# A decoder layer in fp32: partial sums of the first projections added by DVE out of PSUM instead of by POOL, in fewer and larger rounds of k-tiles, with shift and scale made for four k-tiles at a time

## The chip, the cores and the metric

The kernel runs on one core of a Trainium2 chip. The metric is the device time of one execution in microseconds; less is better. The engines are named as the profile names them: PE (matmuls), PEld (its weight loads), DVE (vector), ACT (scalar), POOL (GpSimd) and SP, whose queue issues nearly all loads.

## The reference

One layer (DEPTH is 1) of a decoder trunk over 256 tokens of width 2048. The part around the change:

```python
mod = (jax.nn.silu(c) @ w_ada[l] + b_ada[l]).reshape(B, N_MOD, 1, D)
sh1, sc1, gt1, sh2, sc2, gt2 = (mod[:, j] for j in range(N_MOD))
h = rmsnorm(x, g_mix[l]) * (1.0 + sc1) + sh1
z = h @ w_in[l]          # 2048 x 16392, cut into the inputs of three mixers and three gates
```

c is one vector, so the modulation is a product of a vector with a 2048 x 12288 matrix, 100 MB of which all has to be read; shift sh1 and scale sc1 (33 MB) must be there before h is. The products z feed an mLSTM, a differential attention and a stick-breaking attention; their outputs go through one projection each, are gated and summed, and go through an output projection. A gated MLP with a causal convolution follows. All is fp32, and every large weight matrix is read once.

## The kernel before

**Precision.** PE multiplies in an fp32 format that it rounds (fp32r). Each operand is therefore split into a high part, which ACT makes by a cast (line 305, `hi`), and a low part, which DVE makes as raw minus high (line 307, `lo`); a product takes three matmuls: high by high, high by low, low by high. Every weight tile passes through this split. One split covers two k-tiles: 128 x 1024 elements where a chunk has 512 columns, 128 x 880 where it has 440 ("wide" and "narrow" below). The split tiles have four buffers each, of two k-tiles.

**Modulation.** DVE multiplies each row block of w_ada by its element of silu(c) and accumulates (`ada_mac`, lines 204 and 206); sums over the partitions are then made on PE (`partition_sums`, tile pm, line 218) and DVE. `ada_first(k0)` makes shift and scale for two k-tiles of 128 features: 4 steps, each with two loads of 512 KB (shift and scale side by side in one raw tile) and four accumulations of 512 columns. Then `make_h` builds hh and hl, the split h for these k-tiles, on ACT (lines 400 and 355) and DVE (line 356). The result for k-tiles 0 and 1 comes first, the others run beside the projections.

**Rounds.** The first 13 chunks of columns of w_in (the inputs of the stick-breaking and differential attentions: four chunks of 512 with features on the partitions, "F", line 339; two of 512 and seven of 440 with tokens on the partitions, "T", line 337) are multiplied before all of h is there. So the 16 k-tiles are cut into rounds. `partial(ci, kt0, kt1)` does chunk ci for k-tiles kt0 to kt1: load, split, matmuls into two PSUM banks (`gemm`; there are three banks for it), and the result goes to its place in SBUF. In the first round ACT writes it there (line 464). In later rounds before, ACT copies the bank to a tile `part` (line 461) and POOL adds that to the place (line 466). In the last round, 12 to 16 (8 to 16 for two postponed chunks), DVE adds straight out of PSUM (line 468). The rounds before: 0 to 2 and 2 to 4 for all 13 chunks; 4 to 6 and 6 to 8 for ten; 4 to 8 for the other three; 8 to 12 for eleven; then the last.

**Order.** After each chunk `tick()` advances the queue of modulation steps by `rates["ada"]` (0.4, later 0.9 in this stage) and side work (attention) by another rate. If h for a round is not made when the round is written, `partial` pumps the queue until it is; `drain(ada)` ends it after round 8 to 12. The order on each engine is worked out from this by a planner that simulates times; the engines themselves run their queues in order. Loads of modulation and weights go through SP's one queue in order. Raw tiles of two k-tiles of w_in have three buffers of 512 KB of their own; raw tiles of four k-tiles and those of `ada_first` share three buffers of 1 MB.

After the last round come the gates, the mixers as side work beside the remaining projections, the branches, the output projection and the MLP.

Of the kernel before, what the change touches and what calls it, by code (L numbers as in the profile page):

```python
# [10 lines left out]
F32 = mybir.dt.float32  # L11
F32R = mybir.dt.float32r
AF = mybir.ActivationFunctionType
ALU = mybir.AluOpType
# [3 lines left out]
P = 128  # L18
S = 256
NT = S // P  # L20
D = 2048
KD = D // P
# [17 lines left out]
def kernel(  # L40
# [6 lines left out]
    nc = tc.nc  # L47
    x2d, out2d = x[0], out[0]
    w_ada, w_in, w_out, w_up, w_down = w_ada[0], w_in[0], w_out[0], w_up[0], w_down[0]
# [4 lines left out]
    rawp = ctx.enter_context(tc.tile_pool(name="rawp", bufs=3))  # L54
# [6 lines left out]
    adaps = ctx.enter_context(tc.tile_pool(name="adaps", bufs=1, space=PSUM))  # L61

    def slot(i, name):
        n = NT * MH * (MDH + 1) + 8 if i == 2 else 2048
        return slots.tile([P, n], F32, tag=f"s{i}", name=name)
# [4 lines left out]
    def wide(name):  # L70
        return tmp.tile([P, 512], F32, tag="wide", name=name, bufs=3)
# [7 lines left out]
    V, A, T = nc.vector, nc.scalar, nc.tensor  # L79


    ident = const.tile([P, P], F32, name="ident")
    make_identity(nc, ident)
    ones = const.tile([P, P], F32, name="ones")
# [36 lines left out]
    ccol, gmix_c = colsA[:, 0:16], colsA[:, 16:32]  # L121
    bsh1_c, bsc1_c, bsh2_c, bsc2_c = (colsA[:, 32 + 16 * i:48 + 16 * i] for i in range(4))
# [51 lines left out]
    ada = deque()  # L174
    state = {"ada": 0.0, "side": 0.0, "split": None, "load": None, "hold": None, "h": 0, "started": False}
# [13 lines left out]
    rates = {"ada": 0.0, "side": 1.0}  # L189
# [9 lines left out]
    def ada_mac(accs, raw, kt0, nk):  # L199
        for k in range(nk):  # L200
            kt = kt0 + k
            acc = accs[kt % len(accs)]
            if kt < len(accs):
                V.tensor_scalar(acc, raw[:, k, :], ccol[:, kt:kt + 1], None, ALU.mult)  # L204
            else:
                V.scalar_tensor_tensor(acc, raw[:, k, :], ccol[:, kt:kt + 1], acc, ALU.mult, ALU.add)  # L206

    def partition_sums(accs):

        pm = adaps.tile([P, 512], F32, tag="adaps", name="pm")  # L210
        if len(accs) > 1:
            for i, acc in enumerate(accs):
                for k in range(4):
                    T.matmul(pm[:, k:k + 1], lhsT=acc[:, k * P:(k + 1) * P], rhs=ones[:, 0:1],
                             start=k + i == 0, stop=i == len(accs) - 1, skip_group_check=True)
            return pm
        for k in range(4):
            T.transpose(pm[:, k * P:(k + 1) * P], accs[0][:, k * P:(k + 1) * P], ident)  # L218
        sums = tmp.tile([P, 4], F32, tag="sums", name="sums")
        V.tensor_reduce(sums, pm.rearrange("p (k f) -> p k f", k=4), AX.X, ALU.add)  # L220
        return sums

    def ada_first(k0):

        accs = [adap.tile([P, 512], F32, tag="acc", name="acc", bufs=2)]
        if k0 == 0:
            accs.append(sidewide("acc2"))
        for q in range(4):
            raw = rawp.tile([P, 4, 512], F32, tag="raw", name="raw")
            step = 2 if k0 == 0 and q == 3 else 4  # L230
            for j in range(0, 4, step):
                for i in range(2):
                    r0, c0 = q * 512 + j * P, i * D + k0 * P
                    with tc.issue_after(state["load"].ins) if k0 else nullcontext():
                        load = nc.sync.dma_start(raw[:, j:j + step, i * 256:(i + 1) * 256],
                                                 w_ada[r0:r0 + step * P, c0:c0 + 256].rearrange("(k p) f -> p k f", p=P))
            if k0 == 0:
                state["load"] = load
            with tc.issue_after(state["first"].ins) if k0 == 2 and q == 0 else nullcontext():
                ada_mac(accs, raw, 4 * q, 4)  # L240
            yield
        pm = partition_sums(accs)
        ks = slice(k0, k0 + 2)
        V.tensor_tensor(b1[:, ks], pm[:, 0:2], bsh1_c[:, ks], ALU.add)  # L244
        V.tensor_tensor(a1[:, ks], pm[:, 2:4], bsc1_c[:, ks], ALU.add)
        V.tensor_tensor(a1[:, ks], a1[:, ks], gmix_c[:, ks], ALU.mult)
        make_h(k0, k0 + 2)

    def ada_late(comp, g):

# [10 lines left out]
    def ada_columns(comp, bcol, dst, gcol=None):  # L261
        for g in range(4):
            for acc in ada_late(comp, g):
                yield
            pm = partition_sums([acc])
            ks = slice(4 * g, 4 * g + 4)
            V.tensor_tensor(dst[:, ks], pm[:, 0:4], bcol[:, ks], ALU.add)
            if gcol is not None:
                V.tensor_tensor(dst[:, ks], dst[:, ks], gcol[:, ks], ALU.mult)
# [17 lines left out]
    a1 = const.tile([P, KD], F32, name="a1")  # L287
    b1 = const.tile([P, KD], F32, name="b1")
# [101 lines left out]
    def make_h(kt0, kt1):  # L390
        ts = []
        for kt in range(kt0, kt1):
            t = small("ht")
            ts.append(t)
            if kt0 == 0:
                A.activation(hh[:, kt, :], xnT_k(kt), AF.Identity, scale=a1[:, kt:kt + 1], bias=b1[:, kt:kt + 1])
                V.tensor_scalar(t, xnT_k(kt), a1[:, kt:kt + 1], b1[:, kt:kt + 1], ALU.mult, ALU.add)
                state["split"] = V.tensor_tensor(hl[:, kt, :], t, hh[:, kt, :].bitcast(F32), ALU.subtract)
            else:
                A.activation(t, xnT_k(kt), AF.Identity, scale=a1[:, kt:kt + 1], bias=b1[:, kt:kt + 1])  # L400
                state["split"] = split(hh[:, kt, :], hl[:, kt, :], t)
        if kt0 == 0:
            state["first"] = state["split"]
        state["h"] = kt1
# [44 lines left out]
    def shaped(src, dst):  # L449
        return src.rearrange("p (a b) -> p a b", a=dst.shape[1]) if len(dst.shape) == 3 else src  # L450

    def partial(ci, kt0, kt1, on_pool=True):
        orient, col0, n, dest, scale = first[ci]
        while state["h"] < kt1:
            pump(ada, 1)
        pin = kt0 == 0 and ci == 1
        acc = gemm(orient, hact, w_in, 0, col0, n, kt0, kt1, hold=state["first"] if pin else None, hold_all=pin)
        for b in range(2):
            if kt0 and on_pool:
                t = wide("part")  # L460
                A.activation(t[:, :n], acc[b][:, :n], AF.Copy, scale=scale)  # L461
            for cs, d in dest(b):
                if kt0 == 0:
                    A.activation(d, shaped(acc[b][:, cs], d), AF.Copy, scale=scale)
                elif on_pool:
                    nc.gpsimd.tensor_tensor(d, d, shaped(t[:, cs], d), ALU.add)
                else:
                    V.scalar_tensor_tensor(d, shaped(acc[b][:, cs], d), scale, d, ALU.mult, ALU.add)
        tick()

    NC, NE = 10, 11
    ada.extend(ada_first(k0) for k0 in range(2, KD, 2))
    rates["ada"] = 0.4
    for ci in range(13):
        partial(ci, 0, 2)
    for ci in range(13):
        partial(ci, 2, 4)
    with tc.issue_after(state["load"].ins):
        late_vectors()
    for ci in range(NC):  # L480
        partial(ci, 4, 6)
    for ci in range(NC):
        partial(ci, 6, 8)
    rates["ada"] = 0.9
    for ci in range(NC, 13):
        partial(ci, 4, 8)
    for ci in range(NE):
        partial(ci, 8, 12)
# [305 lines left out]
    ada.append(ada_rest())  # L794
    rates["side"] = 2.4
    for ci in range(13):
        partial(ci, 12 if ci < NE else 8, 16, on_pool=False)
        if ci == 5:
            side.append(stick())

# [18 lines left out]
    for ch in range(2):  # L819
        acc = gemm("T", hact, w_in, 0, C_MO + ch * 512, 512, 0, KD)  # L820
# [5 lines left out]
    for ch in range(2):  # L826
        acc = gemm("T", hact, w_in, 0, C_MV + ch * 512, 512, 0, KD)
# [5 lines left out]
    for t, col0, f0 in ((mqT, C_MQ, 0), (mkT, C_MK, 8)):  # L833
        for ch in range(2):
            acc = gemm("F", hact, w_in, 0, col0 + ch * 512, 512, 0, KD)
# [40 lines left out]
    for ch in range(4):  # L876
        acc = gemm("T", mact, w_out, 0, ch * 512, 512, 0, KD)
        cs = slice(ch * 512, (ch + 1) * 512)
        for tt in range(NT):
            t = wide("t512")  # L880
# [15 lines left out]
        for k2 in range(2):  # L896
            pb = bank("px2")
            for tt in range(NT):
                for j in range(2):
                    k = 4 * ch + 2 * k2 + j  # L900
                    T.transpose(pb[:, j * S + tt * P:j * S + (tt + 1) * P], x2[tt][:, k * P:(k + 1) * P], ident)
            for j in range(2):
                k = 4 * ch + 2 * k2 + j
                A.activation(xT[k // 8][:, (k % 8) * S:(k % 8 + 1) * S], pb[:, j * S:(j + 1) * S], AF.Copy,
                             scale=a2[:, k:k + 1])
# [5 lines left out]
    for k in range(0, KD, 2):  # L911
# [3 lines left out]
        for j in range(2):  # L915
            b = b2[:, k + j:k + j + 1]
# [9 lines left out]
    for half, (c0, c1) in enumerate(((0, 6), (6, NCH))):  # L926
        ath = [slots.tile([P, 8, S], F32R, tag=f"s{i}", name=f"ath{i}") for i in (0, 3, 4)]
        atl = [slots.tile([P, 8, S], F32R, tag=f"s{i}", name=f"atl{i}") for i in (5, 6, 7)]
        for ch in range(c0, c1):
# [18 lines left out]
            i, j0 = (ch - c0) // 2, ((ch - c0) % 2) * 4  # L948
            for b in range(2):
                V.tensor_tensor(y[b], accu[b], y[b], ALU.mult)  # L950
                ks = slice(j0 + 2 * b, j0 + 2 * b + 2)
# [4 lines left out]
        for n in range(4):  # L956
            acc = gemm("T", act, w_down, c0 * 512, n * 512, 512, 0, 4 * (c1 - c0))
            cs = slice(n * 512, (n + 1) * 512)
            for tt in range(NT):
                t = wide("t512")  # L960
# [34 lines left out]
```

## Time and profile before

| | |
|---|---|
| three runs | 1870.74 us median (1869.49 to 1871.23) |
| profiled execution | 1869.62 us, span 1867.8 us, mean granted clock 0.990 |
| PE, weight loads | busy 1799.6 us (96%), 1684.9 us (90%) |
| DVE | busy 1365.7 us (73%) |
| ACT | busy 924.6 us (49%) |
| POOL | busy 180.5 us (10%) |
| DMA | 423.75 MB, 227 GB/s over the span |

The times of the instructions come from the profiled execution, whose own time is 1.8 us more than its span, the distance from its first to its last instruction. Matmuls are pipelined, so that the busy time of PE is more than its work. Idle time of an engine costs only where the engine that sets the pace waits for it.

### The profile page before, as it was taken

To read this page: it belongs to the slowest core of one execution; us is meant where nothing else is said; L and a number is where in the kernel's file an instruction comes from. 1 tells how busy PE (TensorE), PEld (TensorE's weight loads), DVE (VectorE), ACT (ScalarE), POOL (GpSimd) and SP (SyncE) were. 2 spreads that over 40 slices of the span, in tenths; PEclk is the share of its full clock that TensorE was granted. 3 is DMA by queue.
4 is the path that set the end of the run, shared out by engine and by line. 5 is a ranking of instruction groups with operands and counts; after the bars stand their busy time and mean duration, and the time that the engine had idled before them with its cause. 6 is when DMAs were issued, how large, how long until landed. Compare 5 with 4: busy or idle time off the path is not lost.

```text
span 1867.8 us, 30413 instructions
## 1 busy us (share of the span) xinstructions
PE 1799.6 (96%) x12433; PEld 1684.9 (90%) x12433; DVE 1365.7 (73%) x1687; ACT 924.6 (49%) x1226; POOL 180.5 (10%) x146
## 2 busy tenths in 40 slices
PE   6887789999999999999999999999999999999998
PEld 5776679999988999999999879999998889999987
DVE  6999997888888688686887567777774545555554
ACT  6655444666656464453444455444443334444432
POOL 0588652000000000000000000000000000000000
PEclk9988999999999999999999999999999999999999
DMA  9867786667677657666898547777765565555563
GB/s 317 268 211 230 247 273 209 217 231 237 205 254 268 233 187 252 215 235 240 308 306 284 196 151 242 253 249 261 250 212 198 186 197 186 181 181 181 185 221 113
DMA packets 232105, 423.75 MB, mean 227 GB/s; under 512 B 8928, under 2 KB 56349, under 8 KB 231453
## 3 DMA queue, kind: packets, MB, share of 16 engines
q1 hardware_dynamic: 230141, 417.56, 66.4%
q8 instruction: 97, 1.59, 0.4%
q0 software_dynamic: 544, 2.11, 0.3%
q10 hardware_dynamic: 1280, 2.14, 0.3%
q14 instruction: 43, 0.35, 0.1%
HBM read 419.68 MB, written 2.10 MB: 226 GB/s over the span
## 4 chain that ended last, share of the span: by engine, by line
PE 86%; DVE 7%; DMA 3%; issue 2%; ACT 1%; SPq 0%; DVEq 0%; ACTq 0%
PE gp L339 56%; PE gp L337 26%; DVE lo L307 3%; DVE acc L206 3%; DMA raw<-in_w_ada_dram 2%; DMA raw<-in_w_in_dram 1%; ACT hi L305 0%; PE psc L593 0%; DMA x<-in_x_dram 0%; PE pxt L387 0%; PE pm L218 0%; DVE acc L204 0%; ACT x L381 0%; PE pr L284 0%; DVE b L244 0%
## 5 line engine op out<-in xcount | busy, mean ns | idle before, releaser
L307 DVE TENSOR_TENSOR lo<-raw,hi 128x1024 fp32r<-128x1024 f32 (+1 forms) x608 | 760.1, 1261 | 365.4 <-ACT hi L305 346.1
L305 ACT CAST hi<-raw 128x1024 fp32r<-128x1024 f32 (+1 forms) x608 | 622.9, 1037 | 675.9 <-PE gp L339 359.3
L339 PE MATMUL gp<-hh,hi 128*128 128x256 f32 x2688 | 700.1, 285 | 5.9 <-ACT hi L305 2.0
L339 PE MATMUL gp<-hl,hi 128*128 128x256 f32 x2688 | 700.3, 285 | 0.0
L339 PEld LDWEIGHTS gp<-hh,hi 128*128 128x128 f32 x2688 | 519.0, 193 | 8.4 <-ACT hi L305 2.7
L339 PE MATMUL gp<-hh,lo 128*128 128x256 f32 x2688 | 514.8, 284 | 10.5 <-DVE lo L307 10.5
L339 PEld LDWEIGHTS gp<-hl,hi 128*128 128x128 f32 x2688 | 519.6, 193 | 0.7 <-DVE hl L918 0.2
L339 PEld LDWEIGHTS gp<-hh,lo 128*128 128x128 f32 x2688 | 408.2, 193 | 12.3 <-DVE lo L307 11.8
L206 DVE SCALAR_TENSOR_TENSOR acc<-araw,colsA,acc 128x512 f32<-128x512 f32 x240 | 178.9, 745 | 5.7 <-DMA araw<-in_w_ada_dram 3.8
L337 PE MATMUL gp<-hi,hh 128*128 128x440 f32 (+1 forms) x416 | 161.5, 388 | 8.9 <-ACT part L461 4.7
L337 PE MATMUL gp<-hi,hl 128*128 128x440 f32 (+1 forms) x416 | 158.3, 381 | 0.0
L337 PE MATMUL gp<-hi,atl 128*128 128x512 f32 x352 | 136.9, 389 | 0.0
L337 PE MATMUL gp<-hi,ath 128*128 128x512 f32 x352 | 136.9, 389 | 0.0
L206 DVE SCALAR_TENSOR_TENSOR acc<-raw,colsA,acc 128x512 f32<-128x512 f32 x119 | 125.6, 1063 | 6.5 <-DMA raw<-in_w_ada_dram 4.4
L337 PE MATMUL gp<-lo,hh 128*128 128x440 f32 (+1 forms) x416 | 117.2, 384 | 10.3 <-DVE lo L307 10.3
L337 PE MATMUL gp<-lo,ath 128*128 128x512 f32 x352 | 105.8, 389 | 0.0
L337 PEld LDWEIGHTS gp<-hi,hh 128*128 128x128 f32 x416 | 79.9, 192 | 24.9 <-ACT part L461 7.3
L337 PEld LDWEIGHTS gp<-lo,hh 128*128 128x128 f32 x416 | 78.5, 191 | 24.2 <-DVE lo L307 14.1
L337 PEld LDWEIGHTS gp<-hi,hl 128*128 128x128 f32 x416 | 79.8, 192 | 10.0
L337 PEld LDWEIGHTS gp<-lo,ath 128*128 128x128 f32 x352 | 66.1, 188 | 13.8
L337 PEld LDWEIGHTS gp<-hi,ath 128*128 128x128 f32 x352 | 66.1, 188 | 13.7
L337 PEld LDWEIGHTS gp<-hi,atl 128*128 128x128 f32 x352 | 66.1, 188 | 13.7
(338 smaller groups left out, 1746.3 us busy)
## 6 DMA issues: line engine op xcount, KB each, us to landing
raw<-in_w_in_dram SPq DMA_DIRECT2D x92, 1024.0 KB, 5.0
raw<-in_w_up_dram SPq DMA_DIRECT2D x88, 1024.0 KB, 5.0
araw<-in_w_ada_dram SPq DMA_DIRECT2D x128, 512.0 KB, 5.7
raw<-in_w_down_dram SPq DMA_DIRECT2D x44, 1024.0 KB, 4.9
raw<-in_w_ada_dram SPq DMA_DIRECT2D x62, 512.0 KB, 5.6
raw<-in_w_branch_dram SPq DMA_DIRECT2D x24, 1024.0 KB, 5.0
raw<-in_w_out_dram SPq DMA_DIRECT2D x16, 1024.0 KB, 6.0
raw<-in_w_in_dram SPq DMA_DIRECT2D x17, 880.0 KB, 4.6
```

Of the source, the lines that this page charges most:

```text
L206: V.scalar_tensor_tensor(acc, raw[:, k, :], ccol[:, kt:kt + 1], acc, ALU.mult, ALU.add)
L305: A.copy(hi[:, :, :n], raw[:, k0:k0 + 2, :n])
L307: state["split"] = V.tensor_tensor(lo[:, :, :n], raw[:, k0:k0 + 2, :n], hi[:, :, :n].bitcast(F32), ALU.subtract)
L337: T.matmul(o, lhsT=a(s0 + k)[:, sl], rhs=wk[:, :n], **kw)
L339: T.matmul(o, lhsT=wk[:, sl], rhs=a(s0 + k), **kw)
```

## The change

In all rounds after the first, DVE adds the result out of PSUM, as only the last round did; the copies on ACT and the additions on POOL are no more. The rounds are now 0 to 2, 2 to 4 and 4 to 8 for all 13 chunks, 8 to 12 for eleven, and the last as before. Of the modulation, k-tiles 2 and 3 are still made by `ada_first`; the other twelve by the new `ada_quad`, four k-tiles at a time: 8 steps, each with two loads of 512 KB (rows of 2 KB instead of 1 KB) and two accumulations of 1024 columns. The two accumulators take turns in slot s4. Sums over the partitions come from `ada_sums`, by matmuls with a column of ones. The rates are 0.5, 0.45 and 0.63.

```diff
+    def ada_sums(accs, k0, nk):
+
+        pm = adaps.tile([P, 512], F32, tag="adaps", name="pm")
+        for i, acc in enumerate(accs):
+            for k in range(2 * nk):
+                T.matmul(pm[:, k:k + 1], lhsT=acc[:, k * P:(k + 1) * P], rhs=ones[:, 0:1],
+                         start=k + i == 0, stop=i == len(accs) - 1, skip_group_check=True)
+        ks = slice(k0, k0 + nk)
+        V.tensor_tensor(b1[:, ks], pm[:, 0:nk], bsh1_c[:, ks], ALU.add)
+        V.tensor_tensor(a1[:, ks], pm[:, nk:2 * nk], bsc1_c[:, ks], ALU.add)
+        V.tensor_tensor(a1[:, ks], a1[:, ks], gmix_c[:, ks], ALU.mult)
+        make_h(k0, k0 + nk)
...
+    def ada_quad(k0, acc):
+
+        for q in range(8):
+            raw = rawp.tile([P, 2, 1024], F32, tag="raw", name="raw4")
+            for i in range(2):
+                r0, c0 = q * 256, i * D + k0 * P
+                with tc.issue_after(state["load"].ins):
+                    nc.sync.dma_start(raw[:, :, i * 512:(i + 1) * 512],
+                                      w_ada[r0:r0 + 256, c0:c0 + 512].rearrange("(k p) f -> p k f", p=P))
+            ada_mac([acc], raw, 2 * q, 2)
+            yield
+        ada_sums([acc], k0, 4)
...
         for b in range(2):
-            if kt0 and on_pool:
-                t = wide("part")
-                A.activation(t[:, :n], acc[b][:, :n], AF.Copy, scale=scale)
             for cs, d in dest(b):
                 if kt0 == 0:
                     A.activation(d, shaped(acc[b][:, cs], d), AF.Copy, scale=scale)
-                elif on_pool:
-                    nc.gpsimd.tensor_tensor(d, d, shaped(t[:, cs], d), ALU.add)
                 else:
                     V.scalar_tensor_tensor(d, shaped(acc[b][:, cs], d), scale, d, ALU.mult, ALU.add)
...
-    NC, NE = 10, 11
-    ada.extend(ada_first(k0) for k0 in range(2, KD, 2))
-    rates["ada"] = 0.4
+    NE = 11
+    quads = slot(4, "quads")
+    ada.append(ada_first(2))
+    ada.extend(ada_quad(k0, quads[:, (i % 2) * 1024:(i % 2 + 1) * 1024]) for i, k0 in enumerate((4, 8, 12)))
+    rates["ada"] = 0.5
     for ci in range(13):
         partial(ci, 0, 2)
+    rates["ada"] = 0.45
     for ci in range(13):
         partial(ci, 2, 4)
     with tc.issue_after(state["load"].ins):
         late_vectors()
-    for ci in range(NC):
-        partial(ci, 4, 6)
-    for ci in range(NC):
-        partial(ci, 6, 8)
-    rates["ada"] = 0.9
-    for ci in range(NC, 13):
+    rates["ada"] = 0.63
+    for ci in range(13):
         partial(ci, 4, 8)
     for ci in range(NE):
         partial(ci, 8, 12)
```

## Rows read from the trace of the kernel before

**Rows 1.** From the page: the span in 40 equal slices (46.7 us each), a digit for the busy tenths of PE, DVE and POOL in each; and the chain that ended last, its shares by engine.

```profile
PE   6887789999999999999999999999999999999998
...
DVE  6999997888888688686887567777774545555554
...
POOL 0588652000000000000000000000000000000000
...
PE 86%; DVE 7%; DMA 3%; issue 2%; ACT 1%; SPq 0%; DVEq 0%; ACTq 0%
```

**Rows 2.** The timeline of POOL: start us, us, line, tile. The first addition of each round on POOL: rounds 2 to 4, 4 to 6, 6 to 8 and 8 to 12.

```profile
68.28 1.62 POOL L466 TENSOR_TENSOR sqT<-sqT,part 128x512 f32<-128x512 f32 x1 [65.22 <-ACT part L461]
...
119.35 7.30 POOL L466 TENSOR_TENSOR sqT<-sqT,part 128x512 f32<-128x512 f32 x4
...
162.40 7.93 POOL L466 TENSOR_TENSOR sqT<-sqT,part 128x512 f32<-128x512 f32 x4
...
226.21 1.41 POOL L466 TENSOR_TENSOR sqT<-sqT,part 128x512 f32<-128x512 f32 x1 [3.86 <-ACT part L461]
```

**Rows 3.** Busy time of each engine in six stretches, which are the rounds one after the other (0 to 2; 2 to 4; 4 to 6; 6 to 8 with the three chunks of 4 to 8; 8 to 12; the first chunks of 12 to 16): stretch, its us, busy us (and instructions) of PE, its weight loads, DVE, ACT and POOL, then the granted TensorE clock, the share of the DMA engines and GB/s.

```profile
27.00:66.00 39.00, 37.76 (x215) 34.73 (x215) 32.47 (x43) 26.92 (x49) 0.00 (x0) 0.94 0.98 320
66.00:117.00 51.00, 41.59 (x232) 36.66 (x231) 49.24 (x45) 29.12 (x49) 44.16 (x31) 0.93 0.70 218
117.00:162.00 45.00, 34.58 (x183) 31.41 (x182) 44.64 (x35) 21.99 (x36) 37.96 (x26) 0.85 0.72 223
162.00:224.00 62.00, 47.43 (x244) 40.27 (x243) 61.51 (x55) 29.72 (x49) 48.46 (x33) 0.94 0.72 234
224.00:289.70 65.70, 58.94 (x348) 52.09 (x348) 62.29 (x63) 35.91 (x53) 35.40 (x24) 1.00 0.83 277
289.70:347.00 57.30, 57.30 (x360) 53.93 (x360) 40.87 (x55) 24.22 (x28) 4.84 (x5) 1.00 0.55 180
```

**Rows 4.** Groups of DVE instructions between 27 and 66 us (round 0 to 2): line, operation, tiles, shape, count | busy us, mean ns of one | idle before.

```profile
L206 DVE SCALAR_TENSOR_TENSOR acc<-raw,colsA,acc 128x512 f32<-128x512 f32 x20 | 15.0, 749 | 3.0 <-DMA raw<-in_w_ada_dram 2.7
L307 DVE TENSOR_TENSOR lo<-raw,hi 128x1024 fp32r<-128x1024 f32 x7 | 8.5, 1221 | 1.8 <-ACT hi L305 1.8
L307 DVE TENSOR_TENSOR lo<-raw,hi 128x880 fp32r<-128x880 f32 x7 | 7.5, 1071 | 1.5 <-ACT hi L305 1.3
...
L356 DVE TENSOR_TENSOR hl<-ht,hh 128x256 fp32r<-128x256 f32 x2 | 0.8, 419 | 0.0
```

**Rows 5.** The same view between 69 and 289 us (rounds 2 to 4, 4 to 8 and 8 to 12).

```profile
L206 DVE SCALAR_TENSOR_TENSOR acc<-raw,colsA,acc 128x512 f32<-128x512 f32 x83 | 99.6, 1200 | 3.1 <-DMA raw<-in_w_ada_dram 1.5
L307 DVE TENSOR_TENSOR lo<-raw,hi 128x1024 fp32r<-128x1024 f32 x29 | 52.4, 1843 | 1.6 <-ACT hi L305 1.5
L307 DVE TENSOR_TENSOR lo<-raw,hi 128x880 fp32r<-128x880 f32 x31 | 46.0, 1504 | 0.0
L356 DVE TENSOR_TENSOR hl<-ht,hh 128x256 fp32r<-128x256 f32 x12 | 8.2, 690 | 0.7 <-ACT hh L355 0.7
L204 DVE TENSOR_SCALAR acc<-raw,colsA 128x512 f32<-128x512 f32 x5 | 4.6, 912 | 0.0
L220 DVE TENSOR_REDUCE sums<-pm 128x4 f32<-128x512 f32 x6 | 4.1, 680 | 0.0
```

**Rows 6.** The same view between 289.7 and 347 us (the first chunks of round 12 to 16), additions by DVE alone.

```profile
L468 DVE SCALAR_TENSOR_TENSOR sqT<-gp,sqT 128x512 f32<-128x512 f32 x4 | 2.7, 686 | 4.2 <-PE gp L339 4.2
...
L468 DVE SCALAR_TENSOR_TENSOR dq<-gp,dq 128x440 f32<-128x440 f32 x2 | 1.2, 612 | 0.1
...
L468 DVE SCALAR_TENSOR_TENSOR dk<-gp,dk 128x288 f32<-128x288 f32 x2 | 0.9, 446 | 0.0
...
L468 DVE SCALAR_TENSOR_TENSOR dq<-gp,dq 128x152 f32<-128x152 f32 x2 | 0.6, 306 | 0.0
```

**Rows 7.** The chain that ended last, in order of time: start us, us, what, and how many instructions were merged. First the end of round 8 to 12 and the start of round 12 to 16.

```profile
255.94 5.75 DMA raw<-in_w_ada_dram
...
275.33 0.63 PE pm L218 x4
...
289.68 23.04 PE gp L339 x192
...
312.72 10.91 PE gp L337 x48
...
329.73 14.41 PE gp L337 x72
```

**Rows 8.** Groups of ACT instructions between 69 and 289 us, columns as in rows 4.

```profile
L400 ACT ACTIVATE ht<-xnT,b,a 128x256 f32<-128x256 f32 x12 | 6.6, 594 | 9.8 <-DVE a L246 9.8
L355 ACT CAST hh<-ht 128x256 fp32r<-128x256 f32 x12 | 4.6, 399 | 0.0
```

**Rows 9.** The timeline of DVE at the start of round 12 to 16: start us, us, line, tiles, and in brackets the idle time before it and what ended it.

```profile
292.87 0.68 DVE L468 SCALAR_TENSOR_TENSOR sqT<-gp,sqT 128x512 f32<-128x512 f32 x1
295.55 0.69 DVE L468 SCALAR_TENSOR_TENSOR sqT<-gp,sqT 128x512 f32<-128x512 f32 x1 [2.01 <-PE gp L339]
...
301.30 0.69 DVE L468 SCALAR_TENSOR_TENSOR sqT<-gp,sqT 128x512 f32<-128x512 f32 x1 [2.19 <-PE gp L339]
```

**Rows 10.** The instructions of the tile pm (the sums over partitions) between 60 and 300 us: duration ns as minimum/median/maximum; then what their engine waited for before them, us and times.

```profile
L218 PE MATMUL pm<-ident,acc x24: 270/273/476, 90.3 to 275.7; 128*128 128x128 f32 x24
...
  DVE acc L206: 16.0, 6
```

More of the change, by code (lines that the diff above doesn't have):

```diff
@@ L206, in ada_mac, with partition_sums @@
                 V.scalar_tensor_tensor(acc, raw[:, k, :], ccol[:, kt:kt + 1], acc, ALU.mult, ALU.add)
-    def partition_sums(accs):
+    def partition_sums(acc):
         pm = adaps.tile([P, 512], F32, tag="adaps", name="pm")
[L211 to L216, printed above, removed]
         for k in range(4):
-            T.transpose(pm[:, k * P:(k + 1) * P], accs[0][:, k * P:(k + 1) * P], ident)
+            T.transpose(pm[:, k * P:(k + 1) * P], acc[:, k * P:(k + 1) * P], ident)
         sums = tmp.tile([P, 4], F32, tag="sums", name="sums")
@@ L241, in ada_first @@
             yield
[L242 to L247, printed above, removed]
+        ada_sums(accs, k0, 2)
+    def ada_quad(k0, acc):
[9 more added lines that the diff above has]
+        ada_sums([acc], k0, 4)
     def ada_late(comp, g):
@@ L264, in ada_columns @@
                 yield
-            pm = partition_sums([acc])
+            pm = partition_sums(acc)
             ks = slice(4 * g, 4 * g + 4)
@@ L450, in shaped, with partial @@
         return src.rearrange("p (a b) -> p a b", a=dst.shape[1]) if len(dst.shape) == 3 else src
-    def partial(ci, kt0, kt1, on_pool=True):
+    def partial(ci, kt0, kt1):
         orient, col0, n, dest, scale = first[ci]
@@ L796 @@
     for ci in range(13):
-        partial(ci, 12 if ci < NE else 8, 16, on_pool=False)
+        partial(ci, 12 if ci < NE else 8, 16)
         if ci == 5:
```

## The prediction

> **What bounds the kernel now.** I read the page first. The chain that ended last is 86% TensorE (PE) [rows 1], and in the 40 slices PE is at 9 everywhere except in the first six, which are those where DVE stands at 9 (after 6 in the very first) and where POOL works. So the time is a PE-bound remainder that the change does not touch, behind a first stage in which PE has holes. Whatever the change gives, it gives by letting that remainder begin sooner. Next I looked for the borders of the rounds: the first addition of each round on POOL, and, where round 12 to 16 begins, the chain's piece at 289.68 us [rows 2, 7]. Round 0 to 2 ends about 66 us, round 2 to 4 about 117, 4 to 6 about 162, 6 to 8 with the three late chunks about 224, round 8 to 12 at 289.7. Third, the busy time in those stretches [rows 3]: from 66 to 289.7 us (223.7 us) DVE is busy 49.2 + 44.6 + 61.5 + 62.3 = 217.7 us, 97%, DMA has a share of 0.70 to 0.83, and PE is busy 0.76 to 0.9 of the time by records that overlap. DVE sets the pace. Before 66 us DMA does (share 0.98); after 289.7 PE does (busy for all of its 57.3 us).
>
> Then why DVE is so busy: the same instruction has two prices. In round 0 to 2, with POOL idle, a 512-column accumulation takes 749 ns and the splits 1221 and 1071 [rows 4]; between 69 and 289 us they take 1200, 1843 and 1504 [rows 5]. DMA does not explain it, since its share is higher in the cheap stretch. POOL is what differs.
>
> **The change part by part**, for the stretch from 66 us to the start of round 12 to 16.
>
> *Splits.* Rounds 2 to 4, 4 to 8 and 8 to 12 have 13, 26 and 22 of them, before and after: 30 wide, 31 narrow. At the prices without POOL: 30 x 1.22 + 31 x 1.07 = 69.8 us, against 52.4 + 46.0 = 98.4 in the rows (one record short): 29 us less.
>
> *Modulation accumulation.* 28 steps of 1 MB remain 28. At rates 0.5, 0.45 and 0.63, six instead of five fall into round 0 to 2, leaving 22 steps. A step was four 512-column instructions and becomes two of 1024. No row has that width; from the splits a column costs (1221 - 1071) / 144 = 1.04 ns, so I estimate 0.749 + 512 x 0.00104 = 1.28 us. Its bounds are 1.22 (a split, as wide) and 1.50 (two of 512). 44 x 1.28 = 56 us, bounds 54 and 66, against 99.6 + 4.6 = 104 [rows 5].
>
> *Additions.* 92 instructions are new on DVE. Their shape exists in round 12 to 16: 0.69 us for 512 columns, 0.61 for 440, 0.45 for 288, 0.31 for 152 [rows 6]. A round of 13 chunks has 12 x 0.69, 10 x 0.61, 4 x 0.45, 4 x 0.30 and two tiny ones, 17.7 us; round 8 to 12 has 15.2. Sum 50.6 us.
> A 512-column addition out of PSUM took 0.69 us here, the accumulation out of SBUF 0.749 [rows 4, 6]. [...]
>
> *Sums and h.* The 12 subtractions of hl go from 0.69 to 0.42 us [rows 4, 5], 5.0 us in all instead of 8.2; the six reductions (4.1) go; the tiny additions behind them are half as many, and I leave 3 us for them.
>
> New DVE total: 70 + 56 + 51 + 8 = 185 us. At the old busy share of 97% that is a stretch of 190 us.
>
> *What is late next.* PE: a 256-column matmul goes out every 23.04 / 192 = 0.120 us, a 512-column one every 10.91 / 48 = 0.227, a 440-column one every 14.41 / 72 = 0.200 [rows 7]. A k-tile over 13 chunks is 5.8 + 2.7 + 8.4 = 16.9 us; ten k-tiles less the two postponed chunks (9.6) make 159 us. DMA: w_in 29.7 MB and 22 steps 23.1 MB; at the 277 GB/s of round 8 to 12, which fed the same three large buffers, 52.8 MB take 190 us, at the 320 of round 0 to 2, 165 [rows 3]. So DVE (190), DMA (165 to 190) and PE (159) come close together, and I take 190.
>
> *Off the path.* The ACT copies and POOL's 166 us in the stretch vanish; ACT was busy half the time, so this is worth nothing but shorter queues [rows 3]. SP issues 13 w_in loads for k-tiles 4 to 8 instead of 23, and two loads a step as before. The new accumulators lie in a slot that x leaves in the first 25 us and that the stick-breaking output takes only after the stage.
>
> *Waits added.* An addition on DVE waits for PE's last matmul into its bank, with splits and accumulations queued behind it; in round 12 to 16 such holes are 2.0 to 2.2 us before every second addition of a 512-column chunk [rows 9]. Three banks for two-bank chunks leave PE a chunk of slack. I cost this at nothing, because accumulations that are ready can stand in the hole; without them it is the slower rival.
> The shift and scale for four k-tiles come together, just as the next round needs them. The tail is eight small matmuls (0.27 us each, 2.2), three tiny DVE operations, 0.59 + 0.40 on ACT and 0.42 on DVE for the first k-tile [rows 4, 8, 10]: 4 us, in which PE has nothing of the new round. Before, PE sat 16.0 us over six such tails [rows 10]. Bounds for the three new ones: 0 (hidden by the last chunk) and 46 (4, 2.6 of accumulation, 5.75 of load [rows 7] and 3.0 of ACT for k-tiles two to four, thrice). I take 4 beyond what the 190 hold, nearer to the old rows' 2.7 a tail than to the other end.
>
> *Round 0 to 2.* Bound by DMA, it now carries one more step: 1.05 MB / 320 GB/s = 3 us later.
>
> **The sum.** 190 + 4 + 3 = 197 us against 223.7: 27 us less. The profiled execution took 1869.6 us (span 1867.8, and 1.8 around it), 1.1 under the median of 1870.7. 1870.7 - 27 = 1843.7: I say 1843.
>
> **The rivals.**
> *The tails are exposed.* Each round's first matmuls wait for a load, two accumulations, eight matmuls and four k-tiles of h. At 7 us a tail beyond what I count, half of the upper bound, 21 us go: 1865 us. For it: the last pump of each round falls on its last chunk, and the old chain runs through such a load into the pm matmuls [rows 7]. Against: the large buffers prefetch, and the old tails cost 2.7 us each.
> *Nothing else comes late.* DVE alone sets the stretch, is never idle and has its lower bound in the accumulations, and the tails hide: 70 + 54 + 51 + 8 + 3 = 186, 38 us less, 1833. For it: DMA reached 320 GB/s in round 0 to 2, and its old share of 0.7 has DVE as its cause. Against: three engines within 20% of each other rarely hide each other completely.
> *Slower: additions block DVE.* If its order puts an addition ahead of ready splits and the holes of round 12 to 16 appear in all 37 chunks at 2.0 us each [rows 9], 74 us come on top of DVE's 185: 262 with the 3 of round 0 to 2, against 223.7, 1909 us. It decides from (223.7 - 3 - 185) / 37 = 1.0 us a chunk. For it: the holes exist. Against: there DVE is busy 41 of 57 us and short of other work.
> *The prices do not fall.* If DVE is slow for another reason than POOL, splits stay 98, accumulation is 44 x 1.73 = 76, additions add at least 51, the rest (8.2 + 4.1 + 3) 15: 240 us, with the 3 of round 0 to 2 243, 1890 us. The cheap prices at the higher DMA share [rows 3 to 5] leave little for it.
>
> **Chances.** Forecast 0.58, its own range 1836 to 1853; tails exposed 0.15; DVE alone 0.16; additions block 0.09; prices stay 0.02. What a measurement of this kernel can tell from no change is about 0.2%, 3.7 us. Faster by more: 0.58 + 0.16 + 0.11 of the tails' 0.15 = 0.85; within: 0.04, the tails' upper end; slower 0.09 + 0.02 = 0.11. The range takes the forecast, the DVE-only case with some 7 us for what its rows don't show (clock and prefetch in round 0 to 2), and the tails up to their price: 1826 to 1865.
>
> **What would show it.** In the profile after: accumulations near 1.28 us and splits near 1.22 and 1.07 in the whole first stage (right), or near 1.7 to 1.8 (wrong at the root); the first addition of round 12 to 16 near 266 us instead of 292.9 [rows 9]; DMA share over 0.8 there; holes of DVE before the additions under 1 us a chunk; PE idle before the pm matmuls and before each round's first matmul under 4 us. The prediction is wrong if PE idles for DVE's additions, or if the rounds' first matmuls wait more than 8 us for h.

## The result, and the profile after

The changed kernel takes 1847.17 us (median of 4 runs, 1845.87 to 1847.97) against 1870.99 for the kernel before (4 runs): ratio 0.9871, 95% interval 0.9854 to 0.9888. The forecast was 1843 us, the range 1826 to 1865. In the profiled executions the time went from 1869.62 to 1845.87 us, 23.8 us less. Three runs below have one slow execution each (2848 to 4477 us); their medians here are those of the fast ones.

The page of the changed kernel, the same 40 slices and the chain's shares as in [rows 1]:

```profile
PE   6979899999999999999999999999999999999998
...
DVE  6988777888888587786887576777775545555554
...
POOL 0000000000000000000000000000000000000000
...
PE 92%; DVE 4%; DMA 2%; ACT 1%; issue 1%; SPq 0%; DVEq 0%; ACTq 0%
```

POOL is out of the first stage, DVE is at 8 and 7 in four slices where it was at 9, and the chain's share of DVE has fallen from 7% to 4%. The rounds, as busy time by stretch (columns as in [rows 3]): 2 to 4, 4 to 8, 8 to 12, and the first 57.3 us of the last.

```profile
63.70:114.50 50.80, 38.76 (x228) 33.52 (x226) 48.42 (x71) 18.94 (x24) 0.00 (x0) 0.96 0.86 292
114.50:193.60 79.10, 72.22 (x424) 67.92 (x424) 65.50 (x83) 27.77 (x35) 0.00 (x0) 0.93 0.84 282
193.60:260.40 66.80, 62.55 (x377) 58.93 (x377) 53.44 (x70) 24.42 (x31) 0.00 (x0) 0.93 0.77 265
260.40:317.70 57.30, 57.30 (x351) 54.02 (x352) 37.37 (x55) 24.78 (x30) 0.00 (x0) 0.97 0.44 145
```

Round 12 to 16 starts at 260.35 us instead of 289.68: 29.3 us earlier, where 27 were forecast. Two things in these rows are not in the forecast. DVE, which was to set the pace, is busy 48.4 + 65.5 + 53.4 = 167.4 of 196.7 us, 85%. And the granted clock of PE is 0.93 in round 8 to 12 and 0.97 in the first part of the last, where it was 1.00 before; the forecast had no term for the clock.

DVE's prices between 66 and 255 us, to be laid beside [rows 4 to 6]:

```profile
L206 DVE SCALAR_TENSOR_TENSOR quads<-raw,colsA,quads 128x1024 f32<-128x1024 f32 x41 | 52.4, 1278 | 12.3 <-DMA raw<-in_w_ada_dram 12.2
L322 DVE TENSOR_TENSOR lo<-raw,hi 128x1024 fp32r<-128x1024 f32 x30 | 35.9, 1217 | 3.5 <-ACT hi L320 3.5
L322 DVE TENSOR_TENSOR lo<-raw,hi 128x880 fp32r<-128x880 f32 x31 | 32.9, 1067 | 2.7 <-ACT hi L320 2.6
...
L478 DVE SCALAR_TENSOR_TENSOR sqT<-gp,sqT 128x512 f32<-128x512 f32 x11 | 7.5, 685 | 5.4 <-PE gp L354 5.4
```

The splits are back at 1217 and 1067 ns, the 1024-column accumulation costs 1278, an addition 685. So the prices came out as forecast. What is lost stands in the timeline of PE, at the start of rounds 4 to 8, 8 to 12 and 12 to 16 (start us, us, tiles; in brackets the idle time before and what ended it):

```profile
114.45 1.01 PE L354 MATMUL gp<-hh,hi 128*128 128x256 f32 x3 [7.15 <-ACT hh L370]
```

```profile
193.63 1.01 PE L354 MATMUL gp<-hh,hi 128*128 128x256 f32 x3 [6.72 <-ACT hh L370]
```

```profile
260.35 1.01 PE L354 MATMUL gp<-hh,hi 128*128 128x256 f32 x3 [4.21 <-ACT hh L370]
```

PE waits 7.15, 6.72 and 4.21 us for the high part of the next round's h, hh: 18.1 us. At the first of these borders one can see how the wait grows. DVE's timeline:

```profile
108.02 0.14 DVE L226 TENSOR_TENSOR a<-pm,colsA 128x4 f32<-128x4 f32 x1
...
109.01 1.23 DVE L322 TENSOR_TENSOR lo<-raw,hi 128x1024 fp32r<-128x1024 f32 x1 [0.78 <-ACT hi L320]
110.15 0.15 DVE L227 TENSOR_TENSOR a<-a,colsA 128x4 f32<-128x4 f32 x1
```

and ACT's:

```profile
107.93 1.99 ACT L320 CAST hi<-raw 128x1024 fp32r<-128x1024 f32 x2 [2.64 <-DMA raw<-in_w_in_dram]
110.62 1.99 ACT L320 CAST hi<-raw 128x1024 fp32r<-128x1024 f32 x2 [0.70 <-DMA raw<-in_w_in_dram]
112.52 1.58 ACT L415 ACTIVATE ht<-xnT,b,a 128x256 f32<-128x256 f32 x3
114.01 1.00 ACT L370 CAST hh<-ht 128x256 fp32r<-128x256 f32 x3
```

The additions that finish the sums for shift and scale (lines 225 and 226) are on DVE by 108.02 us. The one product that is still missing, scale times g_mix (line 227, 0.15 us), stands behind a split that waits for ACT, whose cast waited for the load of the new round's weights; it runs at 110.15. ACT, too, has the remaining casts of the new weights ahead of `ht`, and it makes three `ht` before the first `hh`. So the first k-tile is there at 114.45. My reading, which no run tests by itself: the order in the engines' queues fits loads that come earlier than these did.

**Where 29.3 us became 23.8.** The chain of the changed kernel, as in [rows 7], and below it two later pieces of the chain of the kernel before:

```profile
260.35 24.87 PE gp L354 x192
285.22 10.91 PE gp L352 x48
...
796.52 51.83 PE gp L354 x432
...
1201.21 54.70 PE gp L354 x456
```

```profile
821.81 51.83 PE gp L339 x432
...
1224.58 54.70 PE gp L339 x456
```

The first 192 matmuls of round 12 to 16 take 24.87 us, against 23.04 before; 1.8 us are gone, and 27.5 remain at the next piece (312.72 - 285.22). At the 432 matmuls of the branches the lead is 821.81 - 796.52 = 25.3, and in the MLP 1224.58 - 1201.21 = 23.4. The last step, 1.9 us, is the clock: around the output projection PE waits alike in both (2.0 and 1.3 us), and the changed kernel's clock falls there. Two stretches of the changed kernel, the second one there:

```profile
115.00:120.00 5.00, 4.81 (x23) 4.52 (x22) 2.83 (x7) 1.01 (x3) 0.00 (x0) 0.50 1.00 338
1075.00:1090.00 15.00, 11.68 (x54) 9.56 (x53) 8.41 (x17) 8.96 (x18) 0.00 (x0) 0.89 0.44 140
```

After the 7.15 us of idle PE the granted clock is 0.50 for the stretch 115 to 120 us, and it is 0.89 at the output projection. In the kernel before, that place had 1.00:

```profile
1100.00:1115.00 15.00, 11.66 (x57) 9.20 (x55) 8.47 (x18) 8.93 (x18) 0.00 (x0) 1.00 0.43 140
```

The fall at the output projection does not follow from the change alone: the run with POOL memsets (below), whose edit lies in the first stage alone, has a clock of 1.00 there, and 402.8 us between the two later pieces (1200.37 - 797.61), as the kernel before; the changed kernel has 404.7. What decides it stays open.

The other 2.2 us went between about 590 and 690 us of the kernel before, in the mixers, without one wait that shows them; a second profile of the changed kernel loses them at the same places, the kernel with DVE's additions alone (below) does not. I did not find their cause.

### The profile page after: what moved, and what is told of

Same layout as the page of the kernel before. It is cut to its first block, busy times and chain, and to the rows that moved or that the text cites. A ratio compares the mean times of both kernels' runs of the same rounds, so it can differ in the third digit from the quotient of the medians.

```text
span 1844.2 us, 30193 instructions
## 1 busy us (share of the span) xinstructions
PE 1795.0 (97%) x12461; PEld 1689.7 (92%) x12461; DVE 1313.8 (71%) x1715; ACT 878.8 (48%) x1132; POOL 9.0 (0%) x30
## 4 chain that ended last, share of the span: by engine, by line
PE 92%; DVE 4%; DMA 2%; ACT 1%; issue 1%; SPq 0%; DVEq 0%; ACTq 0%
PE gp L354 60%; PE gp L352 28%; DVE lo L322 1%; DMA raw<-in_w_in_dram 1%; DMA raw<-in_w_ada_dram 1%; DVE quads L206 1%; PE psc L602 0%; DMA x<-in_x_dram 0%; ACT hi L320 0%; PE pxt L402 0%; ACT x L396 0%; PE px L910 0%; PE pr L299 0%; PE pm L212 0%; PE pdt L587 0%
## 5 line engine op out<-in xcount | busy, mean ns | idle before, releaser
L322 DVE TENSOR_TENSOR lo<-raw,hi 128x1024 fp32r<-128x1024 f32 (+1 forms) x608 | 728.6, 1207 | 367.6 <-ACT hi L320 345.5
L354 PE MATMUL gp<-hh,hi 128*128 128x256 f32 x2688 | 700.7, 286 | 21.3 <-ACT hh L370 18.1
L352 PE MATMUL gp<-hi,hh 128*128 128x440 f32 (+1 forms) x416 | 157.7, 379 | 4.1 <-DVE dq L478 1.7
L206 DVE SCALAR_TENSOR_TENSOR quads<-raw,colsA,quads 128x1024 f32<-128x1024 f32 x45 | 57.5, 1278 | 12.3 <-DMA raw<-in_w_ada_dram 12.2
```

Of the source, the lines that this page charges most:

```text
L322: state["split"] = V.tensor_tensor(lo[:, :, :n], raw[:, k0:k0 + 2, :n], hi[:, :, :n].bitcast(F32), ALU.subtract)
L352: T.matmul(o, lhsT=a(s0 + k)[:, sl], rhs=wk[:, :n], **kw)
L354: T.matmul(o, lhsT=wk[:, sl], rhs=a(s0 + k), **kw)
```

## The experiments

Theory A: POOL's presence made DVE dear, and taking POOL out is the whole gain. Rival B: the larger rounds and the quads carry it. Theory C: the tails at the round borders are time that nothing else would take. Rival D: loads and DVE are the bound, and the tails are only where PE's slack shows.

**One part alone: DVE adds, everything else as before.**

```diff
-    def partial(ci, kt0, kt1, on_pool=True):
+    def partial(ci, kt0, kt1, on_pool=False):
```

> The kernel before with one edit: DVE adds the partial sums of every later round out of PSUM; the seven rounds, the pairs of k-tiles and the rates stay. Theory A (POOL's presence is what made DVE dear; the larger rounds add little): the prices fall at once. 61 splits at 1.22 and 1.07 us are 70 us, 92 accumulations at 0.749 are 69, 116 additions 64, sums and h 12: 215 us of rows. In the changed kernel 185 us of such rows gave 167 us of busy time, so some 194 us busy here; at 97% round 12 to 16 starts near 66 + 200 = 266 us and the time is 1847 to 1856 us. Rival B (the rounds and the quads carry it; additions of a short round cost DVE what the cheaper splits give back): splits at 1.22 all the same, but 1866 us or more.

Measured: 1844.7 us, ratio to before 0.9861, interval 0.9845 to 0.9877. Two of DVE's prices (columns as in [rows 4]):

```profile
L206 DVE SCALAR_TENSOR_TENSOR acc<-raw,colsA,acc 128x512 f32<-128x512 f32 x84 | 62.4, 746 | 1.6 <-DMA raw<-in_w_ada_dram 1.1
L307 DVE TENSOR_TENSOR lo<-raw,hi 128x1024 fp32r<-128x1024 f32 x28 | 33.8, 1217 | 0.3 <-ACT hi L305 0.3
```

The stretch up to round 12 to 16, first here and then in the changed kernel (columns as in [rows 3]):

```profile
66.00:262.50 196.50, 176.51 (x991) 155.78 (x990) 187.88 (x307) 70.17 (x89) 0.00 (x0) 0.96 0.83 272
```

```profile
63.70:260.40 196.70, 173.53 (x1028) 160.37 (x1026) 167.35 (x223) 71.12 (x88) 0.00 (x0) 0.94 0.82 279
```

That is theory A, 2 us better than its range. The prices are those without POOL, and this one edit gives all of the change's gain. The two kernels need the same 196.6 us for the stretch, by different routes: with short rounds and pairs DVE is busy 187.9 us, 96%, and PE waits 4.1 us for hh; with the larger rounds and quads DVE has 20 us less to do, and the borders take them back.

**The same beside the changed kernel on one chip.**

> The kernel before with DVE's additions alone, once more beside the changed kernel on one chip. In its first run DVE was busy 188 of the 196 us from round 2 to 4 to round 12 to 16. If the larger rounds and the quads are worth nothing as they stand (they take 20 us off DVE and give them back at the round borders), its median is 1843 to 1847 us and lies within 4 us of the changed kernel's. If the first run was luck, it is 1851 us or more.

> The changed kernel itself, for the comparison on one chip: 1845 to 1849 us.

Measured: 1845.9 us (0.9865, 0.9849 to 0.9882) and 1846.6 us (0.9873, 0.9857 to 0.9890). The intervals overlap nearly whole: the larger rounds and the quads, at the rates given, are worth nothing that can be measured.

**One part undone: POOL adds again, in the new rounds.**

```diff
             for cs, d in dest(b):
...
-                    V.scalar_tensor_tensor(d, shaped(acc[b][:, cs], d), scale, d, ALU.mult, ALU.add)
+                    nc.gpsimd.tensor_tensor(d, d, shaped(t[:, cs], d), ALU.add)
```

with the copy of the bank to `t` on ACT ahead of it; in the last round DVE adds, as it always did.

> The changed kernel with one part undone: in rounds 2 to 4, 4 to 8 and 8 to 12 ACT copies the bank and POOL adds, as before; the larger rounds, the quads and the rates stay. Theory A: splits are again near 1.5 to 1.85 us and 1024-column accumulations near 1.7 instead of 1.28; DVE busy 98 + 76 + 15 = 189 us of rows without any addition, more than the 167 of the changed kernel, and the time is 1857 to 1866 us. Rival B: the larger rounds and quads carry the gain, and the time stays within 4 us of the changed kernel's 1847.

Measured: 1864.0 us, 0.9964 (0.9951 to 0.9977); round 12 to 16 starts at 279.9. DVE's prices and the stretch:

```profile
L206 DVE SCALAR_TENSOR_TENSOR quads<-raw,colsA,quads 128x1024 f32<-128x1024 f32 x38 | 66.0, 1737 | 12.8 <-DMA raw<-in_w_ada_dram 12.2
L322 DVE TENSOR_TENSOR lo<-raw,hi 128x1024 fp32r<-128x1024 f32 x28 | 44.2, 1620 | 5.4 <-ACT hi L320 5.4
L322 DVE TENSOR_TENSOR lo<-raw,hi 128x880 fp32r<-128x880 f32 x26 | 42.9, 1686 | 5.5 <-ACT hi L320 5.3 <-issue 0.2
```

```profile
63.50:279.90 216.40, 178.62 (x1031) 160.90 (x1029) 176.33 (x131) 107.81 (x162) 143.96 (x92) 0.92 0.75 255
```

The prices are dear again and the time is where theory A put it, 17 us over the changed kernel, although DVE adds nothing. It is busy 176 us, 9 more than with its 92 additions. That is 81% of a stretch 20 us longer, so this run does not part DVE's prices from the longer way over PE, ACT and POOL; the run after the next does. Without POOL's removal, the rounds and quads give some 7 us; with it, nothing.

**One part undone: shift and scale in pairs.**

```diff
-    quads = slot(4, "quads")
-    ada.append(ada_first(2))
-    ada.extend(ada_quad(k0, quads[:, (i % 2) * 1024:(i % 2 + 1) * 1024]) for i, k0 in enumerate((4, 8, 12)))
+    ada.extend(ada_first(k0) for k0 in range(2, KD, 2))
```

> The changed kernel with one part undone: shift and scale of k-tiles 4 to 15 made for two k-tiles at a time again (four loads of 256 columns' width and four accumulations of 512 columns a step); DVE additions, rounds and rates stay. If fewer, wider accumulations matter, DVE's 88 x 0.75 = 66 us against 44 x 1.28 = 56 show in the time, with three more reductions' worth of small work: 1853 to 1858 us. If DVE has slack (it was busy 85% of the stretch in the changed kernel) and the tails at the round borders are what it loses, pairs cost nothing and half of h is ready earlier: 1842 to 1848 us, with less than 4 us of PE idle time before each round's first matmul, against 7.2, 6.7 and 4.2.

Measured: median 1850.43 us of three executions from 1844.4 to 1852.4; ratio 0.9873, interval 0.9847 to 0.9899. The median lies between the two expectations and the executions reach from one almost to the other: this run decides nothing. Its profile shows a 7 us wait of PE for an accumulation of a pair before round 4 to 8, and 4.1 us for hh later, so pairs do not take the tails away by themselves.

**POOL busy with reads that nobody needs.** In the changed kernel, DVE still adding:

```diff
...
                     V.scalar_tensor_tensor(d, shaped(acc[b][:, cs], d), scale, d, ALU.mult, ALU.add)
+                    if dummy and d.shape[-1] > 100:
+                        w = d.shape[-1]
+                        nc.gpsimd.tensor_tensor(dummy[b][:, :w], dummy[b][:, :w], d, ALU.add)
...
```

`dummy` is two scratch tiles, set to zero before the first round and dropped after round 8 to 12.

> The changed kernel with work put in that nothing needs: after each addition of DVE in rounds 2 to 4, 4 to 8 and 8 to 12, POOL adds the sum it wrote to a scratch tile of 512 columns (two tensors read from SBUF, as POOL's additions before); nothing waits for the result. Theory A (a POOL instruction that reads SBUF holds up DVE's two-input instructions): splits go back to 1.5 to 1.8 us and 1024-column accumulations to 1.6 to 1.8, and the time to 1857 to 1868 us, near the 1864 of the run in which POOL and ACT did the adding. Rival E (that run was long for its chain PE to ACT to POOL and its ACT copies, not for DVE's prices): prices stay within 5% of 1.22 and 1.28 and the time within 4 us of 1847.

Measured: 1873.73 us, ratio to before 1.0019 (1.0010 to 1.0029): the whole gain is gone, and a little more, so that the time lies 6 us above the expected range. DVE and POOL, 66 to 255 us:

```profile
L206 DVE SCALAR_TENSOR_TENSOR quads<-raw,colsA,quads 128x1024 f32<-128x1024 f32 x36 | 59.0, 1639 | 5.8 <-DMA raw<-in_w_ada_dram 5.8
L322 DVE TENSOR_TENSOR lo<-raw,hi 128x1024 fp32r<-128x1024 f32 x28 | 47.5, 1718 | 0.3 <-ACT hi L320 0.3
L322 DVE TENSOR_TENSOR lo<-raw,hi 128x880 fp32r<-128x880 f32 x23 | 32.5, 1419 | 0.2 <-ACT hi L320 0.2
...
L478 DVE SCALAR_TENSOR_TENSOR sv<-gp,sv 128x512 f32<-128x512 f32 x11 | 7.5, 679 | 0.0
```

```profile
L481 POOL TENSOR_TENSOR dm<-dm,sqT 128x512 f32<-128x512 f32 x12 | 22.8, 1921 | 90.2 <-DVE sqT L478 90.2
```

Nothing waits for POOL's sums here, no ACT copy is made, and DVE's prices are 1639, 1718 and 1419 ns all the same; it is busy 209.0 of the 222 us from 64 to 286 us, 94%. Rival E, which put the 1864 us down to that longer way and not to the prices, falls. The last DVE row is the surprise: the additions out of PSUM keep their 679 ns beside the same POOL.

**POOL busy with memsets, which read nothing.** After each addition POOL copies one column of the sum, for the pace, and then sets a scratch tile three times.

```diff
...
+                        nc.gpsimd.tensor_scalar(dummy[b][:, 0:1], d[:, 0:1], 1.0, None, ALU.mult)
+                        for _ in range(3):
+                            nc.gpsimd.memset(dummy[b], 0.0)
...
```

> The changed kernel with POOL kept busy without tensors to read: after each addition of DVE in the same rounds POOL copies one column of the sum (for the pace) and then sets a scratch tile of 512 columns three times. Theory A as told (it is reading SBUF that collides): splits and accumulations stay within 10% of 1.22 and 1.28 us, the time within 5 us of 1847. Rival F (any POOL instruction, by its writes, holds up DVE): splits over 1.35 us and 1853 us or more.

Measured: 1848.16 us, 0.9887 (0.9871 to 0.9904).

```profile
L206 DVE SCALAR_TENSOR_TENSOR quads<-raw,colsA,quads 128x1024 f32<-128x1024 f32 x41 | 52.5, 1281 | 13.4 <-DMA raw<-in_w_ada_dram 13.3
L322 DVE TENSOR_TENSOR lo<-raw,hi 128x1024 fp32r<-128x1024 f32 x30 | 36.0, 1220 | 2.4 <-ACT hi L320 2.4
```

```profile
L482 POOL MEMSET dm<- 128x512 f32 x241 | 122.1, 526 | 7.3
```

POOL is busy 122 us with memsets, nearly as long as with its reads (124 us), and the prices of splits and accumulations, which take two tensors from SBUF, do not move. So these are dear beside POOL's additions, which read SBUF, and not beside its memsets. One price does move: the first instruction of a quad (line 204) multiplies one tensor from SBUF by a column of 128 numbers. Its second instance in the changed kernel, and here, where POOL sets memory from 103.03 to 105.89 us and then copies two columns:

```profile
105.50 0.73 DVE L204 TENSOR_SCALAR quads<-raw,colsA 128x1024 f32<-128x1024 f32 x1
```

```profile
104.95 1.48 DVE L204 TENSOR_SCALAR quads<-raw,colsA 128x1024 f32<-128x1024 f32 x1
```

The third took 0.90 us instead of 0.75. So this POOL work is not free for every DVE instruction; there are but three of these among the quads, and the time does not show them. What holds line 204 up where the splits and the accumulations are not, no run here shows.

**Quads earlier.** Only rates are changed.

```diff
-    rates["ada"] = 0.45
+    rates["ada"] = 0.6
...
-    rates["ada"] = 0.63
+    rates["ada"] = 0.68
```

> The changed kernel with the rates of modulation steps 0.45 to 0.6 and 0.63 to 0.68, so that each quad is written two to three chunks before its round begins. Theory C (the tails at the round borders are time that nothing else would take: PE idle 7.2 + 6.7 + 4.2 us and then some us at the lower clock): the three waits of PE for hh fall under 2 us each and the time to 1832 to 1840 us. Rival D (loads and DVE are the bound, and the tails only the place where PE's slack is seen): the waits move into the rounds, and the time stays at 1844 to 1849 us.

Measured: 1835.22 us, 0.9805 (0.9790 to 0.9820), 12 us under the changed kernel. What PE waited for between 100 and 260 us, where its new round 12 to 16 begins, and three stretches:

```profile
PE gp L354 <- DVE hl L371: 2.1, 1, 2.1
PE gp L354 <- ACT hh L370: 2.0, 1, 2.0
```

```profile
250.45 23.03 PE gp L354 x192
```

```profile
63.30:250.40 187.10, 177.05 (x1029) 161.86 (x1028) 166.78 (x223) 73.17 (x92) 0.00 (x0) 0.95 0.83 286
85.00:105.00 20.00, 15.86 (x72) 12.49 (x70) 20.00 (x34) 4.97 (x6) 0.00 (x0) 0.95 0.88 307
105.00:125.00 20.00, 15.84 (x68) 14.57 (x68) 15.61 (x25) 9.07 (x14) 0.00 (x0) 0.54 0.75 262
```

Theory C, in the main. The waits for h at 8 to 12 and 12 to 16 are gone; the start of the last round moved from 260.35 to 250.45, at the full clock. Of the 14 us of waits that went, 9.9 show in that start. At the first border PE still waits twice 2 us, and the stretch around it (105 to 125 us) has a granted clock of 0.54. This kernel and the next, which differs from it by less than the executions do, are the best of the study.

**The first border: is it the late vectors?** Their 14 small loads, transposes and few vector operations stand just there.

```diff
-    with tc.issue_after(state["load"].ins):
-        late_vectors()
     rates["ada"] = 0.68
     for ci in range(13):
         partial(ci, 4, 8)
     for ci in range(NE):
         partial(ci, 8, 12)
+    with tc.issue_after(state["load"].ins):
+        late_vectors()
```

> The kernel of the earlier quads (rates 0.6 and 0.68; 1835 us) with the 14 small loads, transposes and few vector operations of the late vectors moved from the border of rounds 2 to 4 and 4 to 8 to the end of round 8 to 12. If the small loads in SP's queue hold back the loads of the next round's first weights and of the quad's last step at that border (PE idle and at half the clock between 105 and 125 us), 3 to 6 us go: 1829 to 1832 us. If the border is late for DVE (busy all the time from 65 to 105 us in that run), nothing goes: 1833 to 1837 us.

Measured: 1834.78 us, 0.9811 (0.9797 to 0.9826). Nothing went: the small loads are not the cause. DVE is busy for all of the 20 us before the border (85 to 105 us in the row above).

**The first border: less to load before it.** Rounds 0 to 2, 2 to 4, 4 to 6, 6 to 8, 8 to 12; pairs up to k-tile 8, quads after it; rates so that each group is early.

```diff
+    ada.extend(ada_first(k0) for k0 in (2, 4, 6))
+    ada.extend(ada_quad(k0, quads[:, (i % 2) * 1024:(i % 2 + 1) * 1024]) for i, k0 in enumerate((8, 12)))
...
+    rates["ada"] = 0.4
+    for ci in range(13):
+        partial(ci, 4, 6)
+    rates["ada"] = 0.5
+    for ci in range(13):
+        partial(ci, 6, 8)
```

> DVE adds in all rounds; rounds 0 to 2, 2 to 4, 4 to 6 and 6 to 8 for all 13 chunks, then 8 to 12; shift and scale in pairs up to k-tile 8 and in quads for 8 to 12 and 12 to 16; rates 0.45, 0.35, 0.4, 0.5, 0.68, so that every group is written at least two chunks before its round. Against the earlier quads (1835 us, 14 modulation steps before k-tile 4 is used) only 10 steps have to be loaded before round 4 to 6. If the border before k-tile 4 is late for DMA (share 0.9 to 1.0 up to 105 us in the run with earlier quads, PE at half the clock after it), 4 to 7 us go: 1828 to 1831 us, although DVE has 18 us more additions. If DVE's additions weigh more, 1836 to 1843 us.

Measured: 1847.87 us, 0.9877 (0.9861 to 0.9894). A miss, worse than even the expectation in which DVE's additions weigh more. The stretch from 64 us to round 12 to 16 (columns as in [rows 3]):

```profile
64.00:260.80 196.80, 177.79 (x1044) 157.08 (x1042) 186.17 (x275) 73.77 (x92) 0.00 (x0) 1.00 0.85 284
```

Round 12 to 16 starts at 260.80 us, no earlier than in the changed kernel. DVE is busy 186.2 of 196.8 us, 95%, as with the short rounds and DVE's additions (187.9 of 196.5): the additions of the further rounds and the pairs have taken up what the smaller border could give. The first border itself did come right: from 64 to 260 us the clock is 1.00 throughout, and the only wait for h over 2 us is 4.3 us before round 12 to 16. But from 125 to 200 us DVE is busy all of the 75 us. So a border without a wait is worth nothing where DVE pays for it; how to have both stays open.

## Why the prediction was right, point by point

**Two prices, and POOL as their cause.** Right in each number: 1217, 1067 and 1278 ns against 1.22, 1.07 and an estimated 1.28 us. It had been argued from one pair of stretches; the runs with POOL reading and POOL setting memory show it for splits and accumulations.

**Additions at 0.69 us.** Right (685 ns, against 746 for an accumulation of the same width out of SBUF in the run with DVE's additions alone).

**New DVE total 185 us, so a stretch of 190.** The durations add up as forecast, to 183 us in the trace of the changed kernel, but DVE was busy 167.4 us, 85% of the stretch. The step that failed is laying a sum of durations beside a share of busy time. Instructions that follow one another on DVE overlap in the records, as two rows of the changed kernel's timeline show:

```profile
65.13 0.69 DVE L478 SCALAR_TENSOR_TENSOR sqT<-gp,sqT 128x512 f32<-128x512 f32 x1 [0.62 <-PE gp L354]
...
72.19 1.28 DVE L478 SCALAR_TENSOR_TENSOR skT<-gp,skT 128x512 f32<-128x512 f32 x2
```

Two additions end within 1.28 us, 0.1 less than twice 0.69, and busy time counts such an overlap once. Over the 223 instructions it is 15.6 us, 0.07 each. The 97% of the kernel before was such busy time: its 217.7 us are 228 us of durations. DMA was not full either: its share was 0.77 to 0.86. Without PE's three waits the stretch is 178.6 us, 11 less than the 190.

**Tails at 4 us beyond the rest.** Too small: 18.1 us of waits, 14 more, and some us at the lower clock after them. The two errors, 11 us and 14 us, are of one size and of opposite sign, so 190 + 4 us met the measured 196.7 by luck. The rival of the exposed tails named this mechanism, at 7 us a tail, and had its place and nearly its size (18.1 us for three); its total of 1865 us was too high because it set the tails on a stretch that DVE fills. The run with earlier quads, with 14 of the 18 us of waits gone, gives their worth as 12 us; with the 4 us of waits that were forecast its stretch is 187.1 us and not 194.

**Round 0 to 2 ends 3 us later.** Wrong in sign: the first matmul of the next round is at 63.5 us, in the kernel before at 65.2, so 1.7 us earlier. "Bound by DMA" was taken as 320 GB/s, a rate and not a limit. Transfers between 27 and 63 us, before and after:

```profile
DMA packets 8798, 11.44 MB, mean 318 GB/s; under 512 B 366, under 2 KB 7385, under 8 KB 8794
```

```profile
DMA packets 8298, 12.52 MB, mean 348 GB/s; under 512 B 399, under 2 KB 5297, under 8 KB 8294
```

With one more step asked for, DMA moved 12.52 MB in the time of 11.44. The wider rows of the quads are not the reason: the run with pairs moved 12.35 MB there, at 343 GB/s.

**The rivals.** "Additions block DVE" needed holes of 1.0 us a chunk; the DVE rows above show 5.4 us before the additions to sqT, and PE ended no more than 8 us of DVE's idle time in the stretch, 0.2 us a chunk. "The prices do not fall" fell. "Nothing else comes late" at 1833 us is nearly what the earlier quads reached, 1835, but not in its way: there DVE is busy 166.8 of 187.1 us, 89%, and not without idle time.

**The signs.** The first addition of round 12 to 16 is at 266.78 us, where 266 was said, again by two errors: the round began 2.3 us earlier than forecast, and its first matmuls were slower. PE's wait before a round's first matmul was to be under 4 us and was over it at all three borders; none reached the 8 us that would have made the prediction wrong. PE did idle for DVE's additions, which was the other such sign: 3.7 us in four waits, too little to carry the time.

**The remainder untouched.** Not quite: it gave back 1.8 + 2.2 + 1.9 us, the first and the last by the clock, and the last not in every profile.

## What to carry to other kernels

Before counting what an engine is relieved of, look at what it costs the others by being there: POOL's additions were off DVE's list, and still DVE had less to do when it did them itself. Splits cost it 30 us less (98.4 against 68.8) and accumulations of the same width 37 us less (99.6 against 62.4 with the additions alone); that pays for the 64 us of the additions there, and DVE's busy time up to round 12 to 16 went from 217.7 to 187.9 us. When work is grouped larger, move its schedule ahead with it: a group that is written at its round's border is late there by a whole tail. Here 20 us saved on DVE were lost that way, and raising two rates brought 12 us.

## What the runs showed of the hardware that I had not expected

Beside POOL's additions of two SBUF tensors, DVE's instructions with two SBUF tensors cost 1.3 to 1.4 times as much (1419 for 1067 ns, 1718 for 1217, 1639 for 1278), while an addition with one input in PSUM stayed at 679 ns; 122 us of POOL memsets did nothing to either (1220 and 1281 ns; 688 for the addition), but one multiplication of a single SBUF tensor took 1.48 us beside this work instead of 0.73. And an idle stretch of PE cost more than itself in the changed kernel: after 7.15 us without a matmul PE ran at a granted clock of 0.50 from 115 to 120 us, and after 4.21 us the first 192 matmuls took 24.87 us instead of 23.04.
